# Recurrence-gate matmuls as 64x64 blocks on the four quadrants of TensorE, with a half-exchanged copy of the input for the backward direction

## The chip, the cores and the metric

The kernel runs on one core of one Trainium2 chip. The time is device microseconds of one execution of the whole program, given as the median of several runs. One execution was also profiled: its trace gives the span from the first to the last instruction, and each instruction's start, length and waits. The engines are written as in the profile: PE (TensorE matmuls), PEld (its weight loads), DVE (VectorE), ACT (ScalarE), POOL (GpSimd), SP (SyncE, which issues the DMAs here).

## The reference, cut to what matters

The program is one step of a backbone of four layers on 128 prompt tokens and 256 sample tokens, with 1024 channels. Layers 0 and 3 mix tokens with a gated linear recurrence (RG-LRU); layer 1 has a short convolution, layer 2 a pooling mixer. Each mixer is followed by a layer norm, an MLP of width 4096 and another layer norm. What the change touches is the recurrence's two gates:

```python
def rglru_direction(xc, w_a, b_a, w_x, b_x, lam, h0, reverse):
    bsz, T, _ = xc.shape
    xb = xc.reshape(bsz, T, N_LRU_BLOCKS, LRU_BLOCK)
    r = jax.nn.sigmoid(jnp.einsum('btnd,nde->btne', xb, w_a).reshape(bsz, T, D_RNN) + b_a)
    ig = jax.nn.sigmoid(jnp.einsum('btnd,nde->btne', xb, w_x).reshape(bsz, T, D_RNN) + b_x)
    log_a = (-LRU_C * r.astype(jnp.float32)) * jax.nn.softplus(-lam.astype(jnp.float32))
    a = jnp.exp(log_a)
    u = jnp.sqrt(-jnp.expm1(2.0 * log_a)) * (ig * xc).astype(jnp.float32)
    ...
    h, h_last = linear_recurrence(a, u, h0.astype(jnp.float32))

def lru_mixer(x, w_in, conv_w, conv_b, w_a, b_a, w_x, b_x, lam, w_out, h0):
    gate, rec = jnp.split(x @ w_in, 2, axis=-1)
    xc = depthwise_conv(rec, conv_w, LRU_PAD_L, LRU_PAD_R) + conv_b
    h_f, s_f = rglru_direction(xc, w_a[0], ...)
    h_b, s_b = rglru_direction(xc, w_a[1], ...)
    y = jax.nn.gelu(gate) * (h_f + h_b).astype(x.dtype)
    return y @ w_out, ...
```

Every block of 64 channels has its own 64x64 weights, for each of two gates (`w_a`, `w_x`) and two directions. A group of 128 channels holds two blocks.

## The kernel before, in words

Activations are held channel-major: 8 tiles of 128 channels (partitions) by 384 tokens, 388 to 392 columns in the recurrence layers, where pads lie between and around the two sequences. A large weight matrix comes from memory as 128x128 tiles, sixteen to one DMA of 1 MB (`raw`). ACT rounds eight tiles at a time to a high part (`whi`, L1301) and DVE takes the rest (`wlo`, L1307); each tile then makes three matmuls (L198 to L200: high by high, low by high, high by low). Eight such tiles are one weight item. Four buffers of `whi` and `wlo` exist, so a split runs up to three items ahead of PE.

A recurrence layer (`lru`, L847) goes through 16 items of `lin`. Its 16 output tiles have numbers: 8 to 15 are the recurrence input of channel group c = m - 8, 0 to 7 the gelu gate of group m. `ORD_LIN` (L52) gives their order: a head in which 6 (layer 0) or 4 (layer 3) outputs are built side by side, then one output an item. When an output of the first kind is complete, `rec_done` (L867) makes the convolution: ACT multiplies by the first tap (L875), DVE adds three taps (L879), and the result `xc` goes to one of four buffers. When one of the second kind is complete, `gate_done` (L997) makes the gelu with two ACT and two DVE instructions.

`LIN_CUTS` (L57) cuts the 16 items into five parts; after each of the first four parts stands one block of gates, `gates(g)` (L885), for the channel groups 2g and 2g + 1. For each group, direction and gate it makes one f32 matmul of 128x128 by 388 columns (L893) whose stationary tile holds the two 64x64 blocks on its diagonal and zeros beside them, and a tanh on ACT that empties the PSUM bank (L895). The 1024 columns of weights of one block are loaded by SP as one DMA (`lgate`, L1289 issues it). PSUM has 8 banks in rotation (`acc`).

Behind each block `chain(g)` (L909) puts the rest of the recurrence for its two groups on ACT (tau L930, square root L933, exponential L943, rounding L975) and DVE (L916, L936, L947, the scans L955 and L958, L964, L972, L979), with due times counted in ticks of PE's tiles. It ends in `y`, which the output matrix `lout` reads: `ORD_LOUT` first takes the input groups 0 to 5 for five outputs, and then groups 6 and 7. In layer 0, twelve chunks of a matrix-vector product (`gemv`, L342, matmuls L351 on four column strips of 32) are spread between the items.

The order of the instructions on each engine is made by a planner when the program is built: the order of the code is a priority, and among the instructions that the planner holds ready the earliest goes first. At run time each engine keeps to its list.

Of the kernel before, what the change touches and what calls it, by code (L numbers as in the profile page):

```python
# [17 lines left out]
P = 128  # L18
# [21 lines left out]
def ktouter(ms, kts):  # L40
    return [(k, m) for k in kts for m in ms]


def mouter(ms, kts):
    return [(k, m) for m in ms for k in kts]
# [4 lines left out]
ORD_W1B = mouter(range(16, 32), K8)  # L50
ORD_W2 = [mouter(range(8), range(16 * h, 16 * h + 16)) for h in range(2)]
ORD_LIN = [  # L52
    ktouter([8, 9, 0, 1, 2, 3], K8) + mouter([10, 11, 12, 13, 4, 5, 14, 15, 6, 7], K8),
    ktouter([8, 9, 0, 1], K8) + mouter([10, 11, 2, 3, 12, 13, 4, 5, 14, 15, 6, 7], K8),
]
LIN_HEAD = (6, 4)
LIN_CUTS = ((7, 2, 3, 3, 1), (5, 3, 4, 3, 1))  # L57
_early, _late = range(6), (6, 7)
ORD_LOUT = (
    mouter(range(5), _early)  # L60
# [71 lines left out]
def backbone_kernel(ctx, tc, xT, par, crow, wmod0, wmodp, wmodv, w1, w2, lin, lgate, lout, scin, scout, poolw, band, y_out, st_out):  # L132
# [18 lines left out]
    def acc():  # L151
        return psp.tile([P, 512], F32, tag="acc", name=nm("acc"))
# [124 lines left out]
    def lru_col(t, j, c, d):  # L277
        i = (j * C + c) * 2 + d
        return t[:, i : i + 1]
# [567 lines left out]
    def lru(l, j, ng):  # L847
# [3 lines left out]
        def alloc():  # L851
            S["y"] = [hslot(c, LG) for c in range(C)]
            t = scr.tile([P, NSCR], F32, tag="scr", name=nm("lru"))
            at = [0]

            def take(n):
                at[0] += n
                return t[:, at[0] - n : at[0]]

            S["xct"] = [take(LB) for _ in range(4)]  # L860
            S["ring"] = [hraw() for _ in range(8)] + [take(2 * LB) for _ in range(2)]
            S["ggt"] = [take(LB) for _ in range(4)]

        def buf():
            ring[0] += 1
            return S["ring"][ring[0] % len(S["ring"])][:, : 2 * LG]

        def rec_done(c, ps):
            xc = S["xct"][c % 4][:, :LG]
            S["xc", c] = xc  # L870
            w = PCOLS["cw"][0] + (j * C + c) * 4
            cb = PCOLS["cb"][0] + j * C + c

            def conv():
                act.activation(  # L875
                    xc, ps[:, 0:LG], AF.Identity, bias=par_t[:, cb : cb + 1], scale=par_t[:, w : w + 1]
                )
                for k in range(1, 4):
                    vec.scalar_tensor_tensor(  # L879
                        xc, ps[:, k : k + LG], par_t[:, w + k : w + k + 1], xc, op0=ALU.mult, op1=ALU.add  # L880
                    )

            defer(5 if c == 1 else 1, conv)

        def gates(g):  # L885
            def make(i):
                c, d, k = 2 * g + i // 4, (i // 2) % 2, i % 2

                def f(w):
                    if i % 4 == 0:  # L890
                        S["tr", c], S["ti", c] = buf(), buf()
                    ps = acc()[:, :LG]
                    pe.matmul(ps, lhsT=w, rhs=S["xc", c], start=True, stop=True)  # L893
                    dst = S[("tr", "ti")[k], c][:, d * LG : (d + 1) * LG]
                    act.activation(dst, ps, AF.Tanh, scale=0.5, bias=lru_col((bah, bxh)[k], j, c, d))  # L895
                    if i == 7:
                        chain(g)

                return f

            def block(raw):
                for i in range(8):
                    make(i)(raw[:, i * P : (i + 1) * P])
                    if i < 7:
                        tick()

            G(lgate[j, g], block)
# [487 lines left out]
def _layout(i):  # L1395
    a = {k: np.asarray(v) for k, v in i.items()}
    f = np.float32
    r = {}
    x = np.concatenate([a["x_prompt"][0], a["x_sample"][0]], axis=0)
    r["xT"] = np.ascontiguousarray(x.T).reshape(C, P, T)  # L1400

    par = np.zeros((P, NPAR), f)

    def put(name, v):
        s, e = PCOLS[name]
        par[:, s:e] = _flat(v)

    put("cond", np.stack([_fm(a["c_ctx"]), _fm(a["c"][0])], axis=-1))
    put("bmod", _dup(_fm(a["b_mod"])))
    put("bmod0", _dup(_fm(a["b_mod"][0, : 2 * D])))  # L1410
    put("pos", _pos_embed())
    put("lng", _dup(_fm(a["ln_g"])))
    put("lnb", _dup(_fm(a["ln_b"])))
    put("b1", _fm(a["mlp_b1"]))
    put("b2", _dup(_fm(a["mlp_b2"])))
    put("cw", _fm(a["lru_conv_w"]).transpose(0, 1, 3, 2))
    put("cb", _fm(a["lru_conv_b"]))
    put("ba", _fm(a["lru_b_a"]).transpose(0, 1, 3, 2))
    put("bx", _fm(a["lru_b_x"]).transpose(0, 1, 3, 2))
    put("lam", _fm(a["lru_lambda"]).transpose(0, 1, 3, 2))  # L1420
    s0 = _fm(a["state_lru"][0])
    edge = np.zeros((P, 2, C, 2, 3), f)
    edge[:, :, :, 0, 2] = s0[:, :, 0, :]
    put("edge", edge)
    put("h0b", s0[:, :, 1, :])
    put("scw", _fm(a["sc_conv_w"][0]).transpose(0, 2, 1))
    put("psc", _dup(_fm(a["pool_scale"][0])))
    r["par"] = par

    wm = a["w_mod"].reshape(DEPTH, C, P, 6, C, 4, 32)  # L1430
    wp = [wm[l, :, :, s].reshape(4, 2, P, C, 4, 32).transpose(0, 2, 1, 4, 3, 5) for l, s in ORD_MOD_PE]
    r["wmodp"] = np.stack(wp).reshape(len(wp), 4, P, 2048)
    wt = a["w_mod"].reshape(DEPTH, D, 6, 4, 2, P)
    wv = [wt[l, :, s].transpose(1, 3, 2, 0) for l, s in sum(ORD_MOD_DVE, [])]
    r["wmodv"] = np.stack(wv).reshape(len(wv), 4, P, 2 * D)
    crow = np.concatenate([a["c_ctx"], a["c"][0]])
    r["crow"] = np.ascontiguousarray(np.broadcast_to(crow, (P, 2 * D)))
    w0 = wm[0, :, :, :2].reshape(2, 4, P, 2, 4, 2, 4, 32).transpose(4, 0, 2, 1, 6, 3, 5, 7)
    r["wmod0"] = np.ascontiguousarray(w0).reshape(4, 2, P, 2048)
    r["w1"] = np.stack([_pack(w, ORD_W1A + ORD_W1B) for w in a["mlp_w1"]])  # L1440
    r["w2"] = np.stack([_pack(w, ORD_W2[0] + ORD_W2[1]) for w in a["mlp_w2"]])
    r["lin"] = np.stack([_pack(w, o) for w, o in zip(a["lru_w_in"], ORD_LIN)])
    lg = np.zeros((2, 4, P, 2, 2, 2, P), f)
    for q, name in enumerate(("lru_w_a", "lru_w_x")):
        w = a[name].reshape(2, 2, 4, 2, 2, 64, 64)
        for b in range(2):
            lg[:, :, b * 64 : b * 64 + 64, :, :, q, b * 64 : b * 64 + 64] = w[:, :, :, :, b].transpose(0, 2, 4, 3, 1, 5)
    r["lgate"] = lg.reshape(2, 4, P, 1024)
    r["lout"] = np.stack([_pack(w, ORD_LOUT) for w in a["lru_w_out"]])
    r["scin"] = _pack(a["sc_w_in"][0], ORD_SCIN)  # L1450
    r["scout"] = _pack(a["sc_w_out"][0], ORD_OUT)
    pw = np.zeros((D, D), f)
    for g in range(4):
        pw[g * 256 : g * 256 + 256, g * 256 : g * 256 + 256] = a["pool_w"][0, g]
    r["poolw"] = _pack(pw, ORD_POOL)[0]
    r["band"] = _pool_bands()
    return r
# [33 lines left out]
```

## Time and profile before

| | |
|---|---|
| median of 3 runs | 1614.1 us (1613.33 to 1614.62) |
| the profiled execution: its own time | 1614.0 us |
| its span, first to last instruction | 1612.2 us |
| mean granted TensorE clock | 0.998 |
| PE busy | 1566.6 us (97%) |
| DVE busy | 1155.7 us (72%) |
| ACT busy | 750.0 us (47%) |
| the gate matmuls (L893), both layers | 45.1 us busy, 128 passes |

The shares are means over the whole program. The recurrence layers lie at 44 to 171 us and 1195 to 1322 us, and there the three engines stand differently: such stretches have to be read by themselves. A group's line gives its busy time, the mean length of one instruction and the idle time of its engine just ahead of it with what ended it. The program has 64 gate matmuls and the profile 128: each f32 matmul is carried out as two passes, with a weight load each.

### The profile page before, as it was taken

To read this page: it belongs to the slowest core of one execution; us is meant where nothing else is said; L and a number is where in the kernel's file an instruction comes from. 1 tells how busy PE (TensorE), PEld (TensorE's weight loads), DVE (VectorE), ACT (ScalarE), POOL (GpSimd) and SP (SyncE) were. 2 spreads that over 40 slices of the span, in tenths; PEclk is the share of its full clock that TensorE was granted. 3 is DMA by queue.
4 is the path that set the end of the run, shared out by engine and by line. 5 is a ranking of instruction groups with operands and counts; after the bars stand their busy time and mean duration, and the time that the engine had idled before them with its cause. 6 is when DMAs were issued, how large, how long until landed. Compare 5 with 4: busy or idle time off the path is not lost.

```text
span 1612.2 us, 23828 instructions
## 1 busy us (share of the span) xinstructions
PE 1566.6 (97%) x9388; PEld 1499.2 (93%) x9388; DVE 1155.7 (72%) x1804; ACT 750.0 (47%) x1129; POOL 375.4 (23%) x392
## 2 busy tenths in 40 slices
PE   6999999999999999999999999999999999999996
PEld 5778899999999999999998799999988789999996
DVE  5689999974485569994546999974478997534544
ACT  3796643244253346323434553244259946423422
POOL 2112281002320058110052280001431104000043
PEclk9999999999999999999999999999999999999999
DMA  9777467755344445764443457745333444333321
GB/s 348 285 271 277 152 214 260 271 200 192 123 155 159 173 167 183 252 239 163 151 163 131 163 203 261 263 155 209 108 115 104 174 144 141 131 119 117 131 78 40
DMA packets 42592, 289.63 MB, mean 180 GB/s; under 512 B 4848, under 2 KB 7024, under 8 KB 8432
## 3 DMA queue, kind: packets, MB, share of 16 engines
q1 hardware_dynamic: 42480, 288.12, 50.0%
q8 instruction: 73, 1.20, 0.3%
q14 instruction: 39, 0.32, 0.1%
HBM read 286.51 MB, written 1.59 MB: 179 GB/s over the span
## 4 chain that ended last, share of the span: by engine, by line
PE 81%; DVE 10%; ACT 5%; issue 1%; DMA 1%; POOL 0%; SPq 0%; DVEq 0%; ACTq 0%; POOLq 0%
PE acc L199 26%; PE acc L198 26%; PE acc L200 26%; DVE wlo L1307 1%; DVE lru L879 1%; DMA raw<-in_wmod 1%; ACT hidf L930 1%; DVE hidf L958 1%; DVE X L567 1%; ACT L933 1%; ACT hidf L933 1%; DVE hidf L947 1%; DVE X L674 1%; ACT L943 0%; DVE hidf L955 0%
## 5 line engine op out<-in xcount | busy, mean ns | idle before, releaser
L1301 ACT ACTIVATE whi<-raw 128x1024 fp32r<-128x1024 f32 x338 | 356.2, 1056 | 414.9 <-PE acc L200 342.5
L1307 DVE TENSOR_TENSOR wlo<-raw,whi 128x1024 fp32r<-128x1024 f32 x338 | 433.2, 1283 | 155.3 <-ACT whi L1301 154.9
L198 PE MATMUL acc<-h,whi 128*128 128x384 f32 (+2 forms) x1472 | 498.9, 339 | 6.0 <-DVE h L709 5.5
L199 PE MATMUL acc<-h,wlo 128*128 128x384 f32 (+2 forms) x1472 | 498.1, 338 | 0.0
L200 PE MATMUL acc<-h,whi 128*128 128x384 f32 (+2 forms) x1472 | 468.7, 339 | 0.0
L198 PE MATMUL acc<-hid,whi 128*128 128x384 f32 (+1 forms) x1216 | 411.2, 338 | 0.9 <-ACT hid L975 0.9
L200 PE MATMUL acc<-hid,whi 128*128 128x384 f32 (+1 forms) x1216 | 409.9, 337 | 0.8 <-DVE hid L979 0.8
L199 PE MATMUL acc<-hid,wlo 128*128 128x384 f32 (+1 forms) x1216 | 409.2, 336 | 0.0
L198 PEld LDWEIGHTS acc<-h,whi 128*128 128x128 f32 x1472 | 277.0, 188 | 13.5 <-issue 7.8
L199 PEld LDWEIGHTS acc<-h,wlo 128*128 128x128 f32 x1472 | 276.8, 188 | 1.0 <-issue 0.2
L200 PEld LDWEIGHTS acc<-h,whi 128*128 128x128 f32 x1472 | 273.7, 188 | 1.0 <-DVE X L654 0.4
L198 PEld LDWEIGHTS acc<-hid,whi 128*128 128x128 f32 x1216 | 228.4, 188 | 2.4 <-ACT hid L975 1.5
L200 PEld LDWEIGHTS acc<-hid,whi 128*128 128x128 f32 x1216 | 228.2, 188 | 1.5 <-DVE hid L979 1.5
L199 PEld LDWEIGHTS acc<-hid,wlo 128*128 128x128 f32 x1216 | 228.2, 188 | 0.9
L464 DVE SCALAR_TENSOR_TENSOR mac<-mac,silb 128x1024 f32<-128x1024 f32 x176 | 216.2, 1228 | 1.8
L830 ACT ACTIVATE tmp<-acc,par 128x384 f32<-128x384 f32 x128 | 74.1, 579 | 246.0 <-PE acc L200 246.0
L592 POOL TENSOR_TENSOR X<-X,ssb 128x384 f32<-128x384 f32 x40 | 44.1, 1139 | 467.9 <-ACT ssb L590 467.9
L567 DVE SCALAR_TENSOR_TENSOR X<-acc,m,X 128x128 f32<-128x128 f32 (+1 forms) x176 | 65.4, 412 | 114.9 <-PE acc L200 114.9
L832 DVE TENSOR_TENSOR tmp<-tmp 128x384 f32<-128x384 f32 x128 | 72.6, 567 | 101.8 <-ACT tmp L830 101.8
L782 POOL TENSOR_SCALAR X<-X,ag,xbb 128x128 f32<-128x128 f32 x64 | 135.6, 2132 | 0.4
L833 DVE TENSOR_TENSOR hid<-tmp,hid 128x384 fp32r<-128x384 f32 x128 | 72.8, 569 | 0.3
L603 ACT ACTIVATE tmp<-X 128x384 f32<-128x384 f32 x64 | 33.0, 517 | 75.9 <-DVE X L567 61.4
(194 smaller groups left out, 1188.7 us busy)
## 6 DMA issues: line engine op xcount, KB each, us to landing
raw<-in_w SPq DMA_DIRECT2D x128, 1024.0 KB, 4.9
mac<-in_wmodv SPq DMA_DIRECT2D x44, 1024.0 KB, 5.1
raw<-in_wmodp SPq DMA_DIRECT2D x26, 1024.0 KB, 4.9
park<-in_wmodp SPq DMA_DIRECT2D x18, 1024.0 KB, 8.1
raw<-in_lin SPq DMA_DIRECT2D x16, 1024.0 KB, 4.9
raw<-in_scin SPq DMA_DIRECT2D x12, 1024.0 KB, 4.9
raw<-in_wmod SPq DMA_DIRECT2D x8, 1024.0 KB, 7.8
raw<-in_lout SPq DMA_DIRECT2D x8, 1024.0 KB, 5.0
```

What stands on the lines that cost most here:

```text
L198: pe.matmul(ps, lhsT=hi, rhs=xhi, start=first, stop=False)
L199: pe.matmul(ps, lhsT=lo, rhs=xhi, start=False, stop=False)
L200: late = lambda: pe.matmul(ps, lhsT=hi, rhs=xlo, start=False, stop=last)
L464: vec.scalar_tensor_tensor(prod, raw[i % 2][:, D * q : D * q + D], 1.0, silb[:, D * k : D * k + D], op0=ALU.mult, op1=ALU.mult, accum_out= ...
L567: vec.scalar_tensor_tensor(Xt[c][:, o : o + n], ps[:, a:b], col(g, c, k), Xt[c][:, o : o + n], op0=ALU.mult, op1=ALU.add)
L592: (vec if late or fast else gp).tensor_tensor(Xt[i], Xt[i], ssb, op=ALU.subtract)
L782: gp.tensor_scalar(Xt[c][:, a:b], Xt[c][:, a:b], col(g, c, k), col(xb, c, k), op0=ALU.mult, op1=ALU.add)
L830: act.activation(r, ps[:, :T], AF.Relu, bias=par_t[:, i : i + 1])
L832: vec.tensor_tensor(q, r, r, op=ALU.mult)
L833: vec.tensor_tensor(lo, q, hi.bitcast(F32), op=ALU.subtract)
L1301: act.activation(hi, raws[id(raw)][:, i * 1024 : (i + 1) * 1024], AF.Copy)
L1307: vec.tensor_tensor(lo, raws[id(raw)][:, i * 1024 : (i + 1) * 1024], hi.bitcast(F32), op=ALU.subtract)
```

## The change

The stationary tile of a gate is no longer 128x128 with zeros in two quadrants. Each 64x64 block is a matmul by itself on one quadrant of TensorE. The forward direction uses the quadrants (0, 0) and (64, 64). The backward direction uses (0, 64) and (64, 0): its input `xs` is `xc` with the two halves of 64 partitions exchanged, so that the outputs stand on the right partitions. Four matmuls (two directions, two halves) go out in a row, then two tanhs on ACT as before. The exchanged copy is made by two DMAs for each channel group, issued on ACT's queue behind the convolution, into four buffers that lie in `silb` (free in both recurrence layers). A block's weights shrink from 1024 to 512 columns. In the order of the outputs, 14 and 15 are moved ahead, and the first block of gates stands one item later: the parts are 8, 2, 3, 2, 1 items in place of 7, 2, 3, 3, 1 for layer 0, and 6, 3, 4, 2, 1 in place of 5, 3, 4, 3, 1 for layer 3.

```diff
 ORD_LIN = [
-    ktouter([8, 9, 0, 1, 2, 3], K8) + mouter([10, 11, 12, 13, 4, 5, 14, 15, 6, 7], K8),
-    ktouter([8, 9, 0, 1], K8) + mouter([10, 11, 2, 3, 12, 13, 4, 5, 14, 15, 6, 7], K8),
+    ktouter([8, 9, 0, 1, 2, 3], K8) + mouter([10, 11, 12, 13, 14, 4, 15, 5, 6, 7], K8),
+    ktouter([8, 9, 0, 1], K8) + mouter([10, 11, 2, 12, 3, 13, 14, 4, 15, 5, 6, 7], K8),
 ]
-LIN_CUTS = ((7, 2, 3, 3, 1), (5, 3, 4, 3, 1))
+LIN_CUTS = ((8, 2, 3, 2, 1), (6, 3, 4, 2, 1))
...
+            S["xst"] = [silb[:, i * LB : (i + 1) * LB] for i in range(4)]
...
             def conv():
...
+                for a in (0, 64):
+                    nc.scalar.dma_start(xs[a : a + 64], xc[64 - a : 128 - a])
...
-                    ps = acc()[:, :LG]
-                    pe.matmul(ps, lhsT=w, rhs=S["xc", c], start=True, stop=True)
-                    dst = S[("tr", "ti")[k], c][:, d * LG : (d + 1) * LG]
-                    act.activation(dst, ps, AF.Tanh, scale=0.5, bias=lru_col((bah, bxh)[k], j, c, d))
+            def quad(i, w):
+                c, k = 2 * g + i // 2, i % 2
+                if k == 0:
+                    S["tr", c], S["ti", c] = buf(), buf()
+                ps = [acc()[:, :LG] for _ in range(2)]
+                for d in range(2):
+                    x = S[("xc", "xs")[d], c]
+                    for r in (0, 64):
+                        o = 64 - r if d else r
+                        pe.matmul(
+                            ps[d][o : o + 64],
+                            lhsT=w[r : r + 64, 64 * d : 64 * d + 64],
+                            rhs=x[r : r + 64],
+                            start=True,
+                            stop=True,
+                            tile_position=(r, o),
+                        )
+                for d in range(2):
+                    dst = S[("tr", "ti")[k], c][:, d * LG : (d + 1) * LG]
+                    act.activation(dst, ps[d], AF.Tanh, scale=0.5, bias=lru_col((bah, bxh)[k], j, c, d))
...
-    r["lgate"] = lg.reshape(2, 4, P, 1024)
+    r["lgate"] = lg.reshape(2, 4, P, 512)
```

More of the change, by code (lines that the diff above doesn't have):

```diff
@@ L870, in rec_done @@
             S["xc", c] = xc
+            xs = S["xst"][c % 4][:, :LG]
+            S["xs", c] = xs
             w = PCOLS["cw"][0] + (j * C + c) * 4
@@ L881, in conv @@
                     )
+                for a in (0, 64):
+                    nc.scalar.dma_start(xs[a : a + 64], xc[64 - a : 128 - a])
             defer(5 if c == 1 else 1, conv)
         def gates(g):
[L886 to L891, printed above, removed]
-                    ps = acc()[:, :LG]
-                    pe.matmul(ps, lhsT=w, rhs=S["xc", c], start=True, stop=True)
+            def quad(i, w):
[16 more added lines that the diff above has]
+                for d in range(2):
                     dst = S[("tr", "ti")[k], c][:, d * LG : (d + 1) * LG]
[L895 to L899, printed above, removed]
+                    act.activation(dst, ps[d], AF.Tanh, scale=0.5, bias=lru_col((bah, bxh)[k], j, c, d))
+                if i == 3:
+                    chain(g)
             def block(raw):
-                for i in range(8):
-                    make(i)(raw[:, i * P : (i + 1) * P])
-                    if i < 7:
+                for i in range(4):
+                    quad(i, raw[:, i * P : (i + 1) * P])
+                    tick()
+                    if i < 3:
                         tick()
@@ L1442, in _layout @@
     r["lin"] = np.stack([_pack(w, o) for w, o in zip(a["lru_w_in"], ORD_LIN)])
-    lg = np.zeros((2, 4, P, 2, 2, 2, P), f)
+    lg = np.zeros((2, 4, P, 2, 2, 2, 64), f)
     for q, name in enumerate(("lru_w_a", "lru_w_x")):
@@ L1446, in _layout @@
         for b in range(2):
-            lg[:, :, b * 64 : b * 64 + 64, :, :, q, b * 64 : b * 64 + 64] = w[:, :, :, :, b].transpose(0, 2, 4, 3, 1, 5)
-    r["lgate"] = lg.reshape(2, 4, P, 1024)
+            for d in range(2):
+                o = 64 * (b ^ d)
+                lg[:, :, o : o + 64, :, q, d] = w[:, d, :, :, b].transpose(0, 1, 3, 2, 4)
+    r["lgate"] = lg.reshape(2, 4, P, 512)
     r["lout"] = np.stack([_pack(w, ORD_LOUT) for w in a["lru_w_out"]])
```

## The prediction, made blind

> **What bounds the kernel now.** The page puts PE at 97% of the span, so work taken from PE looks like time. The change touches only the two recurrence layers, so the first view to ask is the busy time in their gate stretches: from the first convolution to the moment when the last recurrence output is ready for the output matrix.
>
> ```profile
> core 0: us, PE busy (x) PEld busy (x) DVE busy (x) ACT busy (x) POOL busy (x), PEclk, DMA share, GB/s
> 52.00:149.50 97.50, 95.78 (x594) 75.87 (x592) 83.79 (x123) 84.42 (x128) 18.18 (x43) 1.00 0.72 273
> 1205.00:1299.00 94.00, 90.06 (x450) 80.20 (x448) 83.25 (x117) 83.73 (x128) 14.16 (x41) 1.00 0.43 150
> ```
>
> Here ACT is busy for 84.4 of 97.5 us and 83.7 of 94.0, DVE for 83.8 and 83.3. These are 86 to 89%, not the 47% and 72% of the page: three engines are near their limit together. The next view is the list of waits in the same stretches, since it says which engine the others stand behind. First the earlier stretch, then the later one:
>
> ```profile
> DVE hidf L936 <- ACT hidf L933: 3.6, 1, 3.6
> ...
> ACT hid L975 <- DVE lru L972: 3.4, 3, 2.0
> ...
> DVE lru L936 <- ACT hidf L933: 2.5, 1, 2.5
> DVE hidf L947 <- ACT hidf L943: 2.4, 2, 1.5
> ...
> ACT tmp L1003 <- PE acc L200: 2.0, 1, 2.0
> ACT whi L1301 <- PE acc L200: 2.0, 2, 1.4
> ```
> ```profile
> ACT hid L975 <- DVE lru L972: 4.5, 4, 2.2
> DVE hidf L936 <- ACT hidf L933: 4.0, 2, 3.6
> ...
> DVE hidf L947 <- ACT hidf L943: 3.0, 3, 1.5
> ...
> PE acc L893 <- DVE lru L879: 2.4, 2, 1.7
> ...
> ACT whi L1301 <- PE acc L200: 1.0, 2, 0.7
> ...
> ACT tmp L1009 <- DVE tmp L1006: 0.7, 2, 0.4
> ```
>
> DVE waits for ACT (8.5 us in the earlier stretch, 7.0 in the later), and ACT for DVE (3.4 and 4.5). ACT waits for PE only 2.0 + 2.0 + 1.0 = 5.0 us in both, and in the later stretch the gates on PE wait for the convolution on DVE. The last view is PE's timeline where each layer's output matrix first needs the last two groups (groups 6 and 7):
>
> ```profile
> 150.12 0.45 PE L198 MATMUL acc<-hid,whi 128*128 128x388 f32 x1 [0.31 <-ACT hid L975]
> ```
> ```profile
> 1299.72 0.45 PE L198 MATMUL acc<-hid,whi 128*128 128x388 f32 x1 [0.58 <-ACT hid L975]
> ```
>
> PE comes to this place and waits for the rounding at the end of the chain. A PE that comes sooner waits longer: **what ends last is the chain of ACT and DVE**, with PE half a microsecond behind as its twin.
>
> **The change part by part.** *The gate matmuls.* The rows for PE:
>
> ```profile
> L893 PE MATMUL acc<-lru,raw 128*128 128x388 f32 x128 | 45.1, 497 | 5.7 <-DVE lru L879 3.8 <-ACT whi L1301 1.5 <-DVE lru L1010 0.3
> ...
> L351 PE MATMUL acc<-raw,sil 128*32 128x256 f32 x416 | 26.4, 382 | 0.0
> ```
> ```profile
> 69.41 0.34 PE L199 MATMUL acc<-h,wlo 128*128 128x392 f32 x1
> 69.58 0.34 PE L200 MATMUL acc<-h,whi 128*128 128x392 f32 x1
> 69.85 1.07 PE L351 MATMUL acc<-raw,sil 128*32 128x256 f32 x16
> 70.85 0.45 PE L198 MATMUL acc<-h,whi 128*128 128x392 f32 x1
> 71.14 0.34 PE L199 MATMUL acc<-h,wlo 128*128 128x392 f32 x1
> ```
>
> The 128 passes of the gates keep PE for 45.1 / 128 = 0.352 us each. The matrix-vector matmuls stand on four column strips: 416 passes in 26.4 us are 0.063 us a pass, where one lasts 0.382, so six overlap, and the strips do run together. If the four quadrants do so too, a quad takes its two passes once, 2 x 0.352 = 0.70 us, in place of four passes of 0.352. Then 32 quads are 22.5 us, and 22.6 us of PE are freed. Going into strips costs 69.85 - 69.58 - 0.17 = 0.10 us, and coming out 71.14 - 70.85 - 0.18 = 0.11: 0.21 for each uninterrupted run of quads, 1.7 us for 8 blocks, 3.4 if the planner parts each block in two, as it did in several blocks of before. So PE gets back 19 to 21 us. No row shows tiles of different rows side by side; the bounds are this and none of it (below).
>
> The Trainium skill has a rule against this: "TensorEngine Tiling (Array Packing)", section "Restrictions and Gotchas", says that different row tiles write different PSUM banks and cannot use the same bank at the same time. The two halves of one direction are such a pair, in one bank. The strips of L351 share all rows, so the trace cannot tell; by the rule a quad would go as two pairs, which is the third rival.
>
> *What the freed time is worth.* By the waits, a faster PE ends at most the 5.0 us that ACT waits for it; the rest of the 20 us turns into waits of PE at the output matrix. I take **-5.0**.
>
> *The copies.* Sixteen groups, two DMAs each, on ACT's list right behind the convolution. No engine but SP issues a DMA in before; the nearest rows are SP's issue time and transfers of like size (a pair moves 2 x 64 x 388 x 4 bytes = 199 KB):
>
> ```profile
> L1289 SPq DMA_DIRECT2D raw<-in_lgate x8: 327/328/328, 43.9 to 1255.1; - x8
> ```
> ```profile
> X<-in_xT SPq DMA_DIRECT2D x8, 192.0 KB, 7.9
> out_y<-X SPq DMA_DIRECT2D x8, 192.0 KB, 1.9
> ```
>
> Issue: 32 x 0.328 = 10.5 us at most; nothing where ACT still has queued work to do meanwhile. ACT is busy 88% of these stretches, so I take the other 12%: **+1.3**. Wait: ACT comes to the issue and must stand until DVE has made the third tap; behind it stand the tanhs, splits and the whole chain, and DVE waits for those. The bounds are rows of ACT waiting for DVE: L1009 waits 0.7 us in 8 instructions of the later stretch, 0.09 each; L975 waits 4.5 in 8, 0.56 each. So 16 x 0.09 = 1.4 to 16 x 0.56 = 9.0. The planner puts other work ahead of the issue, as with L1009, but the three taps go between other work on a DVE that is 88% busy, as with L975; I take the middle, 0.3 each: **+4.8**. The landing lies between 1.9 us (quiet queue) and 7.9 (among loads at the start). The order now gives every block one item more between its groups' outputs and its gates, some 4.3 us (24 passes of 0.18), so I take no wait at a landing of 1.9 to 4.3 us and leave 7.9 to the range. The bytes (3.2 MB more, 2.1 MB less in `lgate`) are nothing beside 26 MB in the first stretch alone (97.5 us at 273 GB/s), and `lgate`'s issues on SP stay eight.
>
> *The moved items.* The first block of gates stands one item, 4.3 us, later. ACT has less to do meanwhile, but the block then goes faster:
>
> ```profile
> 1210.89 0.58 ACT L895 ACTIVATE hidf<-acc,bah 128x388 f32<-128x388 f32 x1
> ...
> 1215.98 0.57 ACT L895 ACTIVATE hidf<-acc,bah 128x388 f32<-128x388 f32 x1
> 1216.45 0.58 ACT L895 ACTIVATE hidf<-acc,bxh 128x388 f32<-128x388 f32 x1
> ```
>
> From the first to the eighth tanh there are 5.56 us; at their own pace of 0.47 it would be 3.3, so 2.3 come back, and the convolution of one more group has been done by then, with 0.6 us on ACT and three taps on DVE. What remains, 4.3 - 2.3 - 0.6 = 1.4 us a layer at worst, I take as **0** and keep in the range. Groups 6 and 7 get their convolutions earlier, which ends PE's 2.4 us of waiting for them; that is PE's wait, not the chain's.
>
> *Sum.* -5.0 + 1.3 + 4.8 = +1.1 us on the profiled execution's 1614.0 (span 1612.2 and 1.8 around it), which stands within 0.1 of the median 1614.1: **1615 us, no difference that can be measured** (a run of this kernel tells about 0.2%, 3.2 us, from none). Its own range is 1611 to 1619.
>
> **The rivals.** *A, faster: the freed time is passed on.* The gates' tanhs are paced by PE, one in 0.70 us where they can go at 0.47. If PE hands over eight results in 2.8 us, tau, root and exponential start sooner, and DVE's waits for them shrink. For it: those waits are the longest in both lists, 8.5 + 7.0 = 15.5 us. Against it: in most blocks ACT puts splits and exponentials between the tanhs and is not idle. Half of 15.5 gone gives -7.8, the copies' cost lying in time that was idle anyway: 1606 us.
>
> *B, slower: ACT stands behind the convolutions.* One mechanism, at one place: the copy's issue is next on ACT's list, the third tap is late, and the tanhs wait behind it. With the wait of L975 (0.56) and one of the two issues uncovered (0.33), 16 x 0.89 - 5.0 = +9.2: 1623 us. It decides from (5.0 + 3.2) / 16 = 0.51 us for each group. For it: ACT's busy time is 88% before anything is added, and the chain runs through it. Against it: the waits of L1009.
>
> The Trainium skill, "DMA: Bandwidth & Descriptors", section "Anatomy of one DMA — SWDGE (gpsimd) path", states that DMA engines do not wait on semaphores and that the wait is done by the issuing sequencer. By that, B's wait is real and only its length is open; no run here shows it yet.
>
> *C, the quadrants do not go four at once* (the change does not do what it says). Two at a time, PE spends 45.1 us as before and some 2.5 us on the switches; nothing is gained and ACT pays: 1614.0 + 6.1 + 2.5 = 1623 us. One at a time, 32 x 8 x 0.352 = 90.1 us, 45 more: about 1660.
>
> **How the numbers follow.** Forecast 0.36, A 0.32, B 0.21, C 0.11 (0.03 of it one at a time). The predicted time is 1615. Of the forecast, 0.03 lies below 1611 and 0.04 above 1617; of A, 0.02 lies within 0.2%. Faster by over 0.2%: 0.30 + 0.03 = 0.33. Within: 0.29 + 0.02 = 0.31. Slower: 0.04 + 0.21 + 0.11 = 0.36. The range takes in A with the 5.0 us beside its 7.8 (1601, of which I leave out the last 2) and B with both issues uncovered in most groups (16 x 1.22 - 5.0 = 14.5, 1628, less 1): 1603 to 1627, which leaves out about 0.18.
>
> **What would show it.** The PE group of the gates should have 256 passes and about 22 us busy (45 speaks for C). PE's idle time should appear at the output matrix, behind the rounding L975, some 5 to 9 us a layer. ACT's waits for PE in the stretches should be gone. ACT should show gaps ended by the taps L879 or by a DMA issue: below 0.5 us for each group the forecast stands or A, above it B. The stretch from the first convolution to the last rounding should be as long as before, within 2 us a layer; if both are shorter by 4 or more, with less waiting of DVE for the root and the exponential, A is right. The prediction is wrong in its base if anything outside the two layers moves by over 2 us, or if the planner puts items between the matmuls of one quad.

## The result, and the profile after

The changed kernel takes **1628.1 us** (1625.81 to 1632.21) against 1613.7 us (1613.0 to 1614.62) for the kernel before on the same chip: 14.4 us slower, ratio 1.009, interval 1.0078 to 1.0102. The forecast was 1615, and the range, which ended at 1627, does not hold it. Of the runs below, one execution of pool_copy (3104.7 us) and one of before_copies_sp (4210.1 us) were in a slow state and are left out of the medians.

| | before | after |
|---|---|---|
| profiled span | 1612.2 us | 1625.6 us |
| mean granted TensorE clock | 0.998 | 0.991 |
| first convolution on ACT to last rounding, layer 0 | 97.55 us | 104.19 us |
| the same in layer 3 | 93.92 us | 99.36 us |
| between the two (last rounding to first convolution) | 1055.68 us | 1058.52 us |

The last three rows are differences of starts in ACT's timeline, from these rows of before and of after (start, length, engine, line, operation; in brackets the idle time ahead of it and what ended it):

```profile
51.99 0.68 ACT L875 ACTIVATE lru<-acc,par 128x388 f32<-128x388 f32 x1 [3.56 <-PE acc L200]
149.54 0.53 ACT L975 ACTIVATE hid<-lru 128x388 fp32r<-128x388 f32 x1 [2.32 <-DVE lru L972]
1205.22 0.67 ACT L875 ACTIVATE lru<-acc,par 128x388 f32<-128x388 f32 x1 [2.07 <-PE acc L200]
1299.14 0.53 ACT L975 ACTIVATE hid<-lru 128x388 fp32r<-128x388 f32 x1 [2.60 <-DVE lru L972]
```
```profile
51.12 0.68 ACT L878 ACTIVATE lru<-acc,par 128x388 f32<-128x388 f32 x1 [3.56 <-PE acc L200]
155.31 0.53 ACT L991 ACTIVATE hid<-lru 128x388 fp32r<-128x388 f32 x1 [2.94 <-DVE lru L988]
1213.83 0.68 ACT L878 ACTIVATE lru<-acc,par 128x388 f32<-128x388 f32 x1 [2.06 <-PE acc L200]
1313.19 0.53 ACT L991 ACTIVATE hid<-lru 128x388 fp32r<-128x388 f32 x1 [1.99 <-DVE lru L988]
```

In the changed kernel's lines L878 is the first tap, L882 the other three, L886 the copies, L902 the gate matmuls, L912 their tanh and L991 the rounding. Of the 13.4 us that the profiled execution is longer, 6.6 and 5.4 lie in the two recurrence layers and 2.8 between them; ahead of the first convolution and behind the last rounding it is 1.5 shorter. The stretches from the first convolution to the last rounding, by engine (length, then the busy time of each, and PE's granted clock behind that of POOL):

```profile
core 0: us, PE busy (x) PEld busy (x) DVE busy (x) ACT busy (x) POOL busy (x), PEclk, DMA share, GB/s
51.00:155.50 104.50, 96.08 (x661) 72.22 (x660) 84.10 (x123) 82.18 (x127) 20.18 (x44) 0.95 0.73 256
1213.60:1313.20 99.60, 89.17 (x514) 75.84 (x512) 83.90 (x118) 83.90 (x129) 17.79 (x41) 0.97 0.45 150
```

ACT and DVE do about the work of before (84.4 and 83.7 us on ACT, 83.8 and 83.3 on DVE) in 104.5 and 99.6 us in place of 97.5 and 94.0. ACT's idle time grew from 13.1 and 10.3 us to 22.3 and 15.7. The work is the same; the holes in it are new. And the clock is no longer 1.00.

**The quadrants do go four at once.** PE's timeline inside a block (an x2 is a pair of tiles):

```profile
83.77 0.49 PE L902 MATMUL acc<-lru,raw 64*64 64x388 f32 x2
83.78 0.49 PE L902 MATMUL acc<-silb,raw 64*64 64x388 f32 x2
84.09 0.49 PE L902 MATMUL acc<-lru,raw 64*64 64x388 f32 x2
84.11 0.49 PE L902 MATMUL acc<-silb,raw 64*64 64x388 f32 x2
```

All four tiles of a pass start within 0.02 us, and the next pass 0.32 us later. At this pace 32 quads of two passes would take about 21 us where 45.1 were spent. What PE spends on them in the two stretches is more (length, busy time of PE and of PEld, clock, DMA):

```profile
51.00:155.50 104.50, 19.68 (x128) 5.76 (x128) 0.95 0.73 256
1213.60:1313.20 99.60, 17.97 (x128) 6.09 (x128) 0.97 0.45 150
```

These are 37.7 us for 256 passes, 7.4 less than before: some of the quads run at half clock (below); the rest of the difference was not looked into. Even this saving does not arrive. PE at the end of layer 3 still waits for the rounding, as long as before (0.58 us), and the chain now ends later:

```profile
1313.77 0.45 PE L198 MATMUL acc<-hid,whi 128*128 128x388 f32 x1 [0.58 <-ACT hid L991]
```

Where PE's time went is in the waits (total us, times, longest), of layer 0 and then of layer 3:

```profile
PE acc L902 <- ACT hidf L912: 4.9, 3, 2.3
...
ACT hidf L912 <- PE acc L902: 3.9, 3, 3.2
```
```profile
PE acc L902 <- ACT hidf L912: 8.1, 2, 4.8
```

The quads now wait for the tanhs to empty PSUM banks: 4.9 and 8.1 us of waiting that was not among the waits of before. The copies are ACT's own:

```profile
L886 ACTq DMA_DIRECT2D silb<-lru x32: 468/604/727, 54.8 to 1279.6; - x32
```
```profile
1247.01 0.71 ACT L946 ACTIVATE hidf<-hidf,c8q 128x388 f32<-128x388 f32 x1
1247.46 1.12 ACTq L886 DMA_DIRECT2D silb<-lru  x2
1248.96 0.71 ACT L946 ACTIVATE hidf<-hidf,c8q 128x388 f32<-128x388 f32 x1 [1.24 <-DVE hidf L974]
```
```profile
1264.33 1.12 ACTq L886 DMA_DIRECT2D silb<-lru  x2
1265.50 0.49 ACT L1019 ACTIVATE tmp<-acc 128x388 f32<-128x388 f32 x1 [1.34 <-DVE wlo L1323]
```

ACT's list stands still while it issues: a pair takes 1.12 us, and in the second case the next instruction starts as the pair ends. The brackets put the 1.24 and 1.34 us down to DVE; the DMA rows say what filled most of them. Added up over the trace, 16 idle gaps of ACT hold an issue; they are 12.5 us, 9.5 of them the issue itself, 3.0 the rest (mostly the wait ahead of it).

### The profile page after: what moved, and what is told of

Same layout as the page of the kernel before. It is cut to its first block, busy times and chain, and to the rows that moved or that the text cites. A ratio compares the mean times of both kernels' runs of the same rounds, so it can differ in the third digit from the quotient of the medians.

```text
span 1625.6 us, 24159 instructions
## 1 busy us (share of the span) xinstructions
PE 1566.7 (96%) x9516; PEld 1492.2 (92%) x9516; DVE 1156.2 (71%) x1804; ACT 747.8 (46%) x1127; POOL 386.5 (24%) x392
## 4 chain that ended last, share of the span: by engine, by line
PE 82%; DVE 10%; ACT 5%; issue 1%; DMA 1%; POOL 1%; SPq 0%; ACTq 0%; DVEq 0%
PE acc L199 26%; PE acc L198 26%; PE acc L200 26%; DVE wlo L1323 1%; DMA raw<-in_wmod 1%; DVE X L567 1%; DVE lru L882 1%; ACT hidf L946 1%; DVE hidf L974 1%; ACT whi L1317 1%; DVE hidf L963 1%; ACT L959 1%; ACT L949 1%; ACT hidf L959 1%; DVE hidf L971 1%
## 5 line engine op out<-in xcount | busy, mean ns | idle before, releaser
L200 PE MATMUL acc<-h,whi 128*128 128x384 f32 (+2 forms) x1472 | 469.5, 339 | 0.0
L200 PE MATMUL acc<-hid,whi 128*128 128x384 f32 (+1 forms) x1216 | 411.0, 338 | 0.3 <-DVE hid L995 0.3
L198 PEld LDWEIGHTS acc<-h,whi 128*128 128x128 f32 x1472 | 277.7, 189 | 17.6 <-issue 7.0
L200 PEld LDWEIGHTS acc<-h,whi 128*128 128x128 f32 x1472 | 274.3, 188 | 1.4 <-issue 0.8
L200 PEld LDWEIGHTS acc<-hid,whi 128*128 128x128 f32 x1216 | 228.7, 188 | 1.1 <-DVE hid L995 0.9
L567 DVE SCALAR_TENSOR_TENSOR X<-acc,m,X 128x128 f32<-128x128 f32 (+1 forms) x176 | 65.1, 411 | 114.4 <-PE acc L200 110.7
L420 POOL TENSOR_SCALAR sc<-m 128x16 f32<-128x16 f32 x7 | 5.7, 817 | 265.0 <-DVE m L478 264.9
```

What stands on the lines that cost most here:

```text
L198: pe.matmul(ps, lhsT=hi, rhs=xhi, start=first, stop=False)
L200: late = lambda: pe.matmul(ps, lhsT=hi, rhs=xlo, start=False, stop=last)
L567: vec.scalar_tensor_tensor(Xt[c][:, o : o + n], ps[:, a:b], col(g, c, k), Xt[c][:, o : o + n], op0=ALU.mult, op1=ALU.add)
```

## The experiments

The theories, as the expectations call them or describe them: **T1**, ACT stands at the copies (issue, and wait for the third tap). **T2**, the new order with its later first block. **T3**, the gates wait for the copies to land. **T4**, the half clock that follows stretches in which PE has little to do. **T5**, the 64x64 blocks cost by themselves. All ratios are to the kernel before on the same chip. With each edit the planner also made new lists, which can cost or gain by themselves; where two kernels have the same lists, it is said.

| kernel | median us | against before, us | interval of the ratio |
|---|---|---|---|
| no_copy | 1621.0 | +7.3 | 1.0029 to 1.0059 |
| sp_issue | 1621.6 | +7.9 | 1.0031 to 1.0064 |
| pool_copy | 1621.1 | +7.4 | 1.0030 to 1.0058 |
| before_copies | 1626.0 | +12.2 | 1.0054 to 1.0094 |
| before_copies_sp | 1612.9 | -0.9 | 0.9989 to 1.0008 |
| before_copies_const | 1613.4 | -0.3 | 0.9990 to 1.0009 |
| before_copies_prev | 1620.8 | +7.1 | 1.0031 to 1.0061 |
| order_only | 1622.5 | +8.8 | 1.0043 to 1.0073 |
| cuts_only | 1622.5 | +8.8 | 1.0039 to 1.0072 |
| outputs_only | 1616.4 | +2.7 | 1.0006 to 1.0024 |
| old_order | 1639.5 | +25.8 | 1.0140 to 1.0174 |
| early_last | 1618.5 | +5.4 | 1.0022 to 1.0046 |
| early_two | 1630.2 | +17.1 | 1.0090 to 1.0124 |
| no_copy_old_order | 1619.3 | +5.6 | 1.0021 to 1.0045 |
| diagonal | 1617.1 | +3.4 | 1.0014 to 1.0036 |
| diagonal_apart | 1618.0 | +4.3 | 1.0016 to 1.0035 |
| pool_copy_old_order | 1623.2 | +9.5 | 1.0044 to 1.0077 |
| after_twice | 1647.6 | +33.9 | 1.0195 to 1.0225 |

### The copies (T1)

From the changed kernel, without the copies (the exchange of halves is left out: the backward gates read the input as it stands), with SP as issuer, and with two POOL copies in place of the DMAs:

```diff
-                for a in (0, 64):
-                    nc.scalar.dma_start(xs[a : a + 64], xc[64 - a : 128 - a])
```
```diff
-                    nc.scalar.dma_start(xs[a : a + 64], xc[64 - a : 128 - a])
+                    nc.sync.dma_start(xs[a : a + 64], xc[64 - a : 128 - a])
```
```diff
-                    nc.scalar.dma_start(xs[a : a + 64], xc[64 - a : 128 - a])
+                    gp.tensor_copy(xs[a : a + 64], xc[64 - a : 128 - a])
```

> The changed kernel without the copies: the backward gates read the input as it stands, its halves not exchanged, so no DMA is issued by ACT and nothing waits for one. Theory 1 (ACT is stopped by the copies: the profile of the changed kernel shows 32 issues of 0.47 to 0.73 us, 604 ns in the middle, on the list through which the chain runs): the loss of 14 us goes, 1610 to 1615. Theory 2 (the new order of the outputs and the later first block of gates cost the time): nearly unchanged, 1624 to 1629. Theory 3 (the gates wait for the copies to land): the loss goes too, 1610 to 1616.

> The changed kernel with the copies issued by SP in place of ACT; the gates still wait for them to land. Theory 1: most of the loss goes, 1612 to 1617, unless weight loads are held up behind the copies on SP's list. Theory 2: 1624 to 1629. Theory 3: 1624 to 1630, since the landing is no sooner, and later where SP's list holds it up.

> The changed kernel with the exchange made by two copies on POOL (64 partitions by 388 columns each) in place of the DMAs; POOL is busy for about a fifth of these stretches. Theory 1: 1608 to 1616, by how much the gates then wait for POOL (64x388 at about 1 us each by the rows of 128x384 on POOL, 1.0 to 1.2 us). Theory 2: 1624 to 1629. Theory 3: between, the wait for the exchanged input is about as long as the landing of 2.2 us: 1618 to 1628.

Without the copies 7.1 us are gone (1628.1 - 1621.0); with SP issuing the same copies, 6.5; with POOL, 7.0. The first two results lie in no theory's range: the copies on ACT's queue are one cause, and 7.3 us have another. That of pool_copy lies in T3's, but no_copy, where nothing waits for an exchange, is as fast, and with the same lists on ACT and DVE. SP's issues are about as long as ACT's, but nothing of the chain stands behind them:

```profile
L886 SPq DMA_DIRECT2D silb<-lru x32: 461/563/1182, 56.0 to 1275.9; - x32
```

So by the medians ACT's standing is worth some 6.5 us and the rest of the copies 0.6, within the noise (sp_issue's four executions go from 1618.1 to 1625.0). The landing is not always nothing, though. In the changed kernel's first block of layer 0 it is a piece of the chain that ended last, and a tanh then waits for the quad:

```profile
62.32 6.02 DMA silb<-lru
```
```profile
69.91 0.58 ACT L912 ACTIVATE hidf<-acc,bah 128x388 f32<-128x388 f32 x1 [3.16 <-PE acc L902]
```

This copy landed after 6.0 us, where the median is 2.2, while the DMA engines were fully busy (share 1.01 from 65.1 to 68.5 us). What it costs was not measured by itself.

The same copies were then put into the kernel before, read by nobody, on ACT's queue (before_copies) and on SP's (before_copies_sp):

```diff
+                xs = S["xst"][c % 4][:, :LG]
+                for a in (0, 64):
+                    nc.scalar.dma_start(xs[a : a + 64], xc[64 - a : 128 - a])
```

(`nc.sync` in place of `nc.scalar` for SP.)

> The kernel before, with the 32 copies issued by ACT behind the convolutions and read by nobody. Theory 1: 16 groups x 2 x 0.60 us are 19 us of ACT's list, more than half of it on the path: 1622 to 1630. Theory 2: 1613 to 1616, the order is the old one. Theory 3: 1613 to 1616, nobody waits for the landing.

> The kernel before with the 32 copies issued by SP and read by nobody. If the 12.3 us of the same copies on ACT's queue came from ACT standing at them, this is within 3 us of before: 1613 to 1617. If they came from the transfers themselves, from the tap being read by a DMA, or from another list that the planner made, 1620 or more as on ACT.

12.2 us on ACT, nothing on SP: the price hangs on ACT's queue, so T1 is shown, with the lists that the planner made for each. In the profiled execution of before_copies 1.7 and 7.2 us of it lie in the two layers and 3.7 between them, where no copy is. Two kernels were to part the issue from the wait for the tap: copies on ACT's queue from a constant, and copies of the group before, whose taps are done.

```diff
+                    nc.scalar.dma_start(xs[a : a + 64], par_t[64 - a : 128 - a, NEARLY : NEARLY + LG])
```
```diff
+                old, S["old"] = S.get("old"), xc
+                    nc.scalar.dma_start(xs[a : a + 64], old[64 - a : 128 - a])
```

> The kernel before with 32 copies on ACT's queue at the same places, of the same size, but from a constant, so that they wait for no tap, and read by nobody. If the issue itself (0.6 us each) is the price, most of the 12.3 us stays: 1621 to 1625. If the wait for the third tap is the price, 1614 to 1618.

> The kernel before with 30 copies on ACT's queue, issued behind each group's convolution, but copying the group before it, whose taps are done by then; read by nobody. If ACT's stand at the copies is the issue itself, 1619 to 1625. If it is the wait for the third tap, 1613 to 1617, with ACT's gaps at the issues half as long or less.

The first does not tell: free of any wait, the copies were moved by the planner out of their place (layer 3's to 1063 to 1076 us, where its first convolution stands at 1207). It shows that an issue costs nothing where ACT has time. In the second, 28 copies (the first group of a layer has none before it) stayed among the convolutions, and 7.1 of the 12.2 us stayed with them. So the larger part is ACT standing without its own tap to wait for, as one of the two expectations has it. The other 5 us are not all the wait: in the profiled executions the two layers are 2.6 us shorter than in before_copies, and the stretch between them 3.7, with no half clock there against 6.8 us.

### The order (T2, T3)

The new order alone, then its two halves, in the kernel before:

```diff
-LIN_CUTS = ((7, 2, 3, 3, 1), (5, 3, 4, 3, 1))
+LIN_CUTS = ((8, 2, 3, 2, 1), (6, 3, 4, 2, 1))
```

cuts_only is this; outputs_only is the new `ORD_LIN` with the old cuts; order_only is both. In outputs_only, layer 0's product of group 5 is taken before its gelu is written, so it uses what the buffer held for group 1.

> The kernel before with nothing but the new order of the outputs and the new cuts; gates as before. Theory 2 (the order costs what remains without the copies, 7.3 us): 1619 to 1623. Theory 4 (the remainder is the half clock that follows when PE, freed by the quads, idles: 20.4 us of half clock without the copies, none before its end in the kernel before): 1612 to 1616 with no half clock, since PE keeps its 45 us of gates. Theory 5 (the quads cost it in another way, by more waits for PSUM banks or by the weight loads): 1612 to 1616.

> The kernel before with the new cuts alone (each block of gates one item later where the new cuts say so), the outputs in the old order. If the later first block is what the new order costs, most of the 8.8 us is here: 1619 to 1623. If the order of the outputs is what costs, 1613 to 1616.

> The kernel before with the new order of the outputs alone, the old cuts. If the later first block is what the new order costs, 1613 to 1616. If the order of the outputs (convolutions of 14 and 15 earlier, gelus later) is what costs, 1619 to 1623.

The cuts alone cost as much as both, 8.8 us; the outputs alone 2.7, 0.4 above their range. The cuts move the first three blocks one item later each and leave the fourth; no run moved the first alone. ACT's timeline of cuts_only in layer 3, and then two rows of before (first convolution, first tanh, first tanh of the fourth block, sixth and last rounding):

```profile
1206.66 0.67 ACT L875 ACTIVATE lru<-acc,par 128x388 f32<-128x388 f32 x1 [2.04 <-PE acc L200]
1217.26 0.57 ACT L895 ACTIVATE hidf<-acc,bah 128x388 f32<-128x388 f32 x1
1275.91 0.57 ACT L895 ACTIVATE hidf<-acc,bah 128x388 f32<-128x388 f32 x1
1290.11 0.51 ACT L975 ACTIVATE hid<-lru 128x388 fp32r<-128x388 f32 x1
1305.52 0.53 ACT L975 ACTIVATE hid<-lru 128x388 fp32r<-128x388 f32 x1 [3.02 <-DVE lru L972]
```
```profile
1272.41 0.57 ACT L895 ACTIVATE hidf<-acc,bah 128x388 f32<-128x388 f32 x1
1281.56 0.52 ACT L975 ACTIVATE hid<-lru 128x388 fp32r<-128x388 f32 x1
```

The first tanh comes 10.60 us after the first convolution, before 5.67 (1210.89 - 1205.22): 4.9 later. The last rounding comes 98.86 us after it, before 93.92: 4.9 later. The two are equal, but the delay does not simply last: at the first tanh of the fourth block it is down to 2.1 us (69.25 against 67.19), and then the sixth rounding comes 7.1 later (83.45 against 76.34). Two things stand there. The new cuts leave two items between the third and the fourth block in place of three, so the third block's chain and the fourth's tanhs stand closer together; and from 1275.9 to 1282.7 us PE has half clock. No run parts them. In layer 0 the first tanh is 5.5 us later and the last rounding only 0.7. Of the rest 2.5 us lie between the layers (1058.15 us against 1055.68), with 6.8 us of half clock, and 1.1 behind layer 3; why is open.

Then the whole change with the old order, to see what the new one is good for:

> The whole change with the order and the cuts of before, the copies on ACT's queue as in the change. If the costs added, the order's 8.8 us would come back: 1619. If they do not add (without copies the old order gave back only 1.7 us), 1624 to 1627. If the extra item between an output and its gates was needed to cover the landing of the copies (the gates would wait for them), no faster than the changed kernel: 1628 or more, with PE waiting at the gates for a DMA.

1639.5 us, 11.4 slower than with the new order. What ended the idle time of the gate matmuls and their weight loads, here and then in the changed kernel (us, times):

```profile
  DMA silb<-lru: 31.0, 17
```
```profile
  DMA silb<-lru: 3.3, 6
```

One of these waits in PE's timeline, and what it does to ACT:

```profile
70.19 0.87 PE L902 MATMUL acc<-silb,raw 64*64 64x388 f32 x1 [7.20 <-DMA silb<-lru]
```
```profile
71.88 0.58 ACT L912 ACTIVATE hidf<-acc,bah 128x388 f32<-128x388 f32 x1 [5.97 <-PE acc L902]
```

So T3 is right for the old order. In the new one the extra item between an output and its gates covers most landings, the first block of layer 0 (above) not. It is a price paid for the copies.

Whether earlier blocks would gain was tried on the kernel before, with cuts of 7, 2, 3, 2, 2 and 5, 3, 4, 2, 2 (early_last), and of 7, 2, 2, 3, 2 and 5, 3, 3, 3, 2 (early_two):

> The kernel before with the last block of gates one item earlier, cuts of 7, 2, 3, 2, 2 and 5, 3, 4, 2, 2. If a block's place sets the end of the layer (a later first block cost 8.8 us), an earlier last one gains: 1606 to 1612. If the chain of ACT and DVE is full from the first block on, so that only a later start counts, 1613 to 1620.

> The kernel before with the last two blocks of gates one item earlier, cuts of 7, 2, 2, 3, 2 and 5, 3, 3, 3, 2. By the place of the blocks, faster by 2 to 10 us: 1604 to 1612. If the chain is full from the first block on, 1613 to 1620.

Neither gains. early_last makes the layers 1.7 and 0.2 us shorter by the measure of the table above, and loses 3.5 us between them and 2.7 behind layer 3: as it would if a rounding that ends sooner met a PE with as much left to do, which was not looked into. early_two is slower than either expectation: in its profiled execution 5.0 us lie between the layers and 7.4 behind layer 3. Why was not followed. No version tried beats the kernel before by more than the noise.

### The quads (T4, T5)

Without copies (the exchange of halves left out), in the old order: the quads alone.

> The quads alone: the old order and cuts, no copies, the backward gates read the input with its halves not exchanged. Theory 2: 1612 to 1615, or below, the order being gone. Theory 4: 1618 to 1622, with stretches of half clock behind windows of 3.4 us in which PE is busy for less than about 1.75 us. Theory 5: 1618 to 1622 without them.

5.6 us slower, in the range of T4 and T5, where the freed time should have shown unmixed. PE's timeline at the last block of layer 3, of this kernel and then of before:

```profile
1274.52 2.87 PE L900 MATMUL acc<-lru,raw 64*64 64x388 f32 x16 [3.95 <-ACT whi L1315]
1279.01 2.22 PE L900 MATMUL acc<-lru,raw 64*64 64x388 f32 x12 [1.63 <-DVE lru L882]
```
```profile
1275.59 2.87 PE L893 MATMUL acc<-lru,raw 128*128 128x388 f32 x8 [1.69 <-DVE lru L879]
```

The quads wait for a split and then for the same taps as before; a shorter matmul behind an input that comes no sooner ends no sooner by much. Next, both directions on the diagonal quadrants (nothing exchanged, all computed), two tiles at once, so that PE spends as long as before; and the same with each direction's tanh right behind it, as before:

```diff
-                        o = 64 - r if d else r
+                        o = r
```
```diff
-            def quad(i, w):
+            def one(i, raw):
+                c, d, k = 2 * g + i // 4, (i // 2) % 2, i % 2
...
+                for r in (0, 64):
+                    pe.matmul(
+                        ps[r : r + 64],
+                        lhsT=raw[r : r + 64, at : at + 64],
+                        rhs=S["xc", c][r : r + 64],
+                        start=True,
+                        stop=True,
+                        tile_position=(r, r),
+                    )
+                act.activation(dst, ps, AF.Tanh, scale=0.5, bias=lru_col((bah, bxh)[k], j, c, d))
```

> The quads with both directions on the quadrants (0, 0) and (64, 64), in the old order, without copies; the weights lie as before by half, and each quad now takes its passes in four rounds instead of two, so PE is not freed (about 42 us for the gates). Theory 4: 1612 to 1616 and no or little half clock, since PE keeps its time. Theory 5: as the quads alone, 1618 to 1622. If the pairs run one after the other instead of together, some 40 us more.

> The kernel before with each gate matmul as two 64x64 blocks on the diagonal quadrants, each followed by its tanh in the order of before (not two directions together). If the grouping into quads costs the 3.4 us that the two directions together on the diagonal cost, this is as before: 1612 to 1616. If the blocks themselves cost it (changes of the array's partition, more instructions), 1616 to 1620.

3.4 and 4.3 us. The first lies between the ranges of T4 and T5. Yet diagonal against no_copy_old_order is the cleanest pair of all: PE, ACT, DVE and POOL have the same lists in both, and only the quadrants of the backward gates differ. The gates on PE, first in diagonal and then in no_copy_old_order (busy time and mean of one; idle time ahead and what ended it):

```profile
L900 PE MATMUL acc<-lru,raw 64*64 64x388 f32 x256 | 44.5, 491 | 7.6 <-DVE lru L882 5.1 <-ACT whi L1315 2.5
```
```profile
L900 PE MATMUL acc<-lru,raw 64*64 64x388 f32 x256 | 30.8, 568 | 18.5 <-DVE lru L882 11.4 <-ACT whi L1315 4.0 <-ACT hidf L910 1.6
```

Of the 13.7 us that PE is freed of, 10.9 come back as idle time ahead of the same matmuls, and the layers are as long (99.0 and 95.4 us, then 99.0 and 95.9). The median with the freed time is even 2.3 us higher, though the intervals overlap. So the freed time of PE, with the half clock that comes with it (below), is worth nothing here, and this is shown. The grouping is not what costs either: diagonal_apart, without it, is no faster. A small cost stays with the blocks themselves (T5), spread in diagonal_apart over 1.5 us in layer 0, 1.0 in layer 3, 1.5 between and 1.0 behind (it starts 1.1 sooner); between the layers and behind them stands a stretch of 3.4 us at half clock each, in the layers none. Its cause is open.

The half clock (T4) is in the windows. The changed kernel, in pairs: a stretch of 3.4 us, and the next one.

```profile
core 0: us, PE busy (x) PEld busy (x) DVE busy (x) ACT busy (x) POOL busy (x), PEclk, DMA share, GB/s
65.10:68.50 3.40, 0.99 (x7) 0.34 (x10) 2.55 (x4) 1.53 (x3) 0.00 (x0) 1.00 1.01 348
68.50:71.90 3.40, 3.40 (x16) 0.98 (x20) 0.00 (x0) 1.35 (x3) 0.00 (x0) 0.50 0.99 339
147.00:150.40 3.40, 1.42 (x9) 1.10 (x8) 3.40 (x6) 3.07 (x4) 1.66 (x6) 1.00 0.28 118
150.40:153.80 3.40, 3.40 (x12) 3.40 (x11) 3.40 (x6) 0.53 (x1) 1.44 (x2) 0.50 0.79 260
174.30:177.70 3.40, 0.61 (x2) 0.47 (x3) 3.40 (x9) 1.04 (x2) 0.00 (x0) 1.00 0.65 272
177.70:181.10 3.40, 3.40 (x7) 1.69 (x6) 0.10 (x1) 0.93 (x2) 0.00 (x0) 0.50 0.00 0
```

The kernel before, where it is nearest to that:

```profile
1274.10:1277.50 3.40, 1.91 (x6) 1.24 (x7) 3.40 (x5) 3.24 (x7) 0.95 (x2) 1.00 0.00 0
1277.50:1280.90 3.40, 3.40 (x18) 2.99 (x18) 3.32 (x7) 3.02 (x6) 1.36 (x3) 1.00 0.73 226
```

The three stretches of the changed kernel with 1.42 us or less of PE are followed by one at half clock, that of before with 1.91 us is not. The busy time alone does not decide it: a stretch of quads in the changed kernel, as busy as the second above, is followed by full clock:

```profile
1266.60:1270.00 3.40, 1.44 (x12) 0.60 (x12) 3.40 (x6) 2.38 (x5) 0.46 (x3) 1.00 0.26 79
1270.00:1273.40 3.40, 2.80 (x17) 2.72 (x16) 3.40 (x6) 2.69 (x6) 3.13 (x2) 1.00 0.92 268
```

What does decide it is open. The pair behind 177.7 us lies between the layers, and may be part of the 2.8 us found there. Over the four runs of the changed kernel the time follows the mean clock: 0.993, 0.991, 0.989 and 0.987 with 1625.8, 1627.4, 1628.8 and 1632.2 us. That fits a price of about 1 us for each such stretch, but it is a correlation, and a longer execution can as well be the one in which PE idles more. Between the layers, where no gate runs, the 13 profiled executions with half clock take 1056.8 to 1059.4 us and six of the seven without it 1055.6 to 1056.9 (early_two 1060.7). Inside the layers no_copy_old_order has 17 us of half clock, diagonal with the same lists none, and they are as long: a price there could only be hidden by a gain from the freed time. The test of it, every quad issued twice in the changed kernel:

```diff
-                for d in range(2):
+                for d in (0, 1, 0, 1):
```

> The changed kernel with every quad of matmuls issued twice, so that PE spends on the gates what it spent before (about 45 us). If PE's half-clock windows cost time and the freed PE time is worth nothing, it is faster than the changed kernel by 1 to 5 us (1623 to 1627), with a mean clock of 0.994 or more. If PE's time in these stretches counts, it is slower: 1632 to 1650. If neither counts, 1628.

1647.6 us is in the range for "PE's time in these stretches counts". The reading is not that simple. The planner, seeing twice the matmuls, gave ACT and DVE other lists, in layer 0 tanhs wait 6.4 us for PE (one of them 4.8) in place of 3.9, and the mean clock stayed at 0.990. A second issue also delays each pair of tanhs by two passes, 32 x 0.65 = 21 us if none of it is hidden, near the 19.5 us measured. So this run does not settle T4, and it does not part the other lists from the later quads.

Last, the whole change in the old order with POOL making the exchange, as what one would ship:

> The whole change but with the old order and with the exchange on POOL. If order and ACT's issue are the two causes (theories 1 and 2): 1610 to 1615. Theory 4: 1617 to 1623, as with the new order. In the old order the gates stand one item sooner behind the convolution, so waits of PE for POOL's copies can add up to 2 us a block.

1623.2 us: better than the change by 4.9, still worse than before, and at the upper end of what T4 gave, not where T1 and T2 alone would put it.

## Why the prediction was wrong

What held: the reading that PE is not what ends last in these layers; the quadrants at once; the bytes as nothing. The quads' 22 us held as a pace (0.65 us a quad), not as PE's busy time of 37.7. The landing without a wait held in layer 3 but not in the first block of layer 0, where it took 6.0 us. The steps can be added up along one path: the quads alone are +5.6 in place of -5.0, the order on top of them +1.7 (7.3 - 5.6) in place of 0, the copies on top of both +7.1 in place of 6.1. Together they are the 14.4, and most of the miss is the first. Along the other path, the order first, it is 8.8 for the order and then 1.5 gained by the quads, which is within the noise. Step by step:

- **The freed time, taken as -5.0.** This is the step that failed. With nothing else changed it came out as +5.6 (no_copy_old_order). The step took the waits of ACT for PE as time that a faster gate gives back. But the 5.0 us were waits for the large matmuls (L200). For the gates themselves ACT waited only 1.0 us in the kernel before, 0.6 in layer 0 and 0.4 in layer 3:

```profile
ACT hidf L895 <- PE acc L893: 0.6, 2, 0.4
```
```profile
ACT hidf L895 <- PE acc L893: 0.4, 1, 0.4
```

A faster gate only moved PE's idle time: not to the output matrix, where 5 to 9 us a layer were expected and 0.58 are seen, but ahead of the quads themselves, behind taps and splits (18.5 us idle in no_copy_old_order against 7.6 in diagonal) and tanhs (4.9 and 8.1 us in the changed kernel). The prediction also had nothing of the half clock that follows some stretches with little PE; its price inside the layers is not shown. Why the quads alone cost 5.6 us is open; 3.4 come with the 64x64 blocks even where PE's time is kept (diagonal).
- **The copies, 1.3 + 4.8 = 6.1.** The size was near, 7.1 measured (1628.1 - 1621.0), and by luck: the parts were not. Issue was taken from SP's row of another DMA, 0.328 us, and covered to 88% by the share of ACT's busy time; it is 0.604 us and 9.5 of the 17.6 us of issue lie in gaps of ACT. The share of busy time of a stretch does not say how much of an added instruction is hidden: the copies are placed behind the convolutions, where the chain needs ACT next. The wait was taken as 4.8 and is 3.0 in the gaps. Nor is a gap of ACT a price yet: 12.5 us of gaps stand against 7.1 us of time.
- **The moved items, taken as 0.** This failed too: 8.8 us alone, 1.7 with the quads. The step counted the first block alone, 4.3 us of delay with 2.3 given back for faster tanhs and 0.6 for work done ahead. By the fourth block of layer 3 of cuts_only 2.8 of 4.9 us had indeed come back; the loss arises behind it, where the third and the fourth block now stand closer. The step did not price the other blocks.
- **The sum.** Order and quads together cost 7.3 us without copies (no_copy), less than 8.8 and 5.6 singly; with the copies' 7.1 these are the 14.4. The terms do not add singly; that each delays the same chain would explain it and is not shown.
- **The rivals.** A fell: both layers became longer, not shorter. C fell. B was the nearest: ACT's gaps at the copies are 12.5 us / 16 = 0.78 us for each group, above its 0.51, and that ACT's standing costs time is what before_copies against before_copies_sp shows, though more of it is issue than wait. But its price counted the -5.0, and it did not have the order's part. The sign named "base wrong" came true: 2.8 us outside the layers.

## What to carry to other kernels

Where two engines carry a chain at nearly 90%, price a change by what it puts into those engines' lists and by where every block of the chain comes to stand; time freed on a third engine is worth nothing until a run shows it. A DMA on a compute engine's queue stops that engine while it issues: give it to an engine that nobody waits for. If a copy needs cover for its landing, the cover is part of its price (here 8.8 us of later blocks in the kernel before, 1.7 with the quads).

## What the runs showed of the hardware

- **PE need not be idle to lose its clock.** Stretches of 3.4 us with 0.99 and 1.42 us of PE were followed by 3.4 us at a granted clock of 0.50; one with 1.91 us was not, and neither was one with 1.44 us of quads. The Trainium skill, "TensorE: Matmul & The Clock Gate", section "Part 1: The HAM clock gate (the "warmup" mystery)", gives a free-running window of 3413 ns and names an idle window as what brings the half clock back; the trace agrees with the length (3.4 us at 0.50), and shows that a window 42% busy (1.42 of 3.4 us) can be enough.
- **Four tiles of 64x64 run side by side, the two row halves of one direction in the same PSUM bank.** Their passes started within 0.02 us of each other and 0.32 us apart. The rule of the Trainium skill, "TensorEngine Tiling (Array Packing)", section "Restrictions and Gotchas", that the prediction weighed would have made two turns of each pass; here it does not hold for two tiles that write different partitions of a bank.
- **A copy of 64x388 f32 from SBUF to SBUF takes its issuer 0.56 to 0.60 us in the median**, on ACT's queue (0.604) as on SP's (0.563), where the 128x1024 load of before took SP 0.328.
